# A list scheduler inside a kernel gets exact footprints, traced lengths, a shared port and another choice among ready instructions

## The chip, the cores and the metric

The kernel runs on one core of a Trainium2 chip. Five engines work side by side, each through its own queue, strictly in the order in which its instructions stand there: TensorE (PE, matrix products and the 128x128 transposes that are written as products), VectorE (DVE), ScalarE (ACT), GpSimd (POOL), and SyncE (SP), which here only issues transfers. An instruction that depends on another engine waits at the head of its queue for a semaphore, and what stands behind it waits with it. The metric is the device time of one execution in microseconds (us).

## What is computed

A first block of two layers and a second block of two layers, on 256 rows of width 1024, all in float32. The first block's layers have a mixer (layer 0: a dilated attention beside a gated linear recurrence, called RG-LRU; layer 1: pooling), an attention to 256 memory rows, and an MLP of width 4096. The second block's layers are, cut to what matters here:

```python
for l in range(DEPTH):
    h = x + 0.5 * swiglu(rms_norm_2(x, ffn1_norm[l]), ffn1_w1[l], ffn1_w3[l], ffn1_w2[l])
    n = rms_norm_2(h, mix_norm[l])
    p = n @ w_in[l]
    u_conv, q, k, v, q_mem = jnp.split(p, splits, axis=-1)
    y_conv = conv_module(u_conv, conv_w[l], conv_b[l], conv_ln_g[l], conv_ln_b[l])
    ...
    y_swa = sliding_window_attention(q, k, v, swa_sinks[l])
    ...
    y_mem = memory_attention(qm, mk, mv)
    y = jnp.concatenate([y_conv, y_swa, y_mem], axis=-1)
    h = h + y @ w_out[l]
    h = h + 0.5 * swiglu(rms_norm_2(h, ffn2_norm[l]), ffn2_w1[l], ffn2_w3[l], ffn2_w2[l])
    x = rms_norm_2(h, final_norm[l])

def conv_module(u, w_dw, b_dw, ln_g, ln_b):
    a, gate = jnp.split(u, 2, axis=-1)
    y = a * jax.nn.sigmoid(gate)
    y = lax.conv_general_dilated(
        y, w_dw[:, None, :], window_strides=(1,),
        padding=[(CONV_WIDTH_2 - 1, 0)],
        dimension_numbers=('NWC', 'WIO', 'NWC'),
        feature_group_count=CONV_CH) + b_dw
    y = layer_norm(y, ln_g, ln_b)
    return jax.nn.silu(y)
```

The convolution is depthwise, with 31 taps over 384 channels; q and k are normed and get rope. The part between `p = n @ w_in[l]` and `y @ w_out[l]` is called the mixer of the second block below; it occurs twice, for l = 0 and l = 1.

## The kernel before, in words

Every large product runs on PE in three terms. A float32 weight arrives by DMA as `raw`, ACT rounds it to `hi` (L303), DVE takes the rest `lo` = raw - hi (L304), and activations are split the same way (`h`, `put`, L367 on ACT and L368 on DVE). A product of a 128x128 block with 512 columns is then three matmuls, L325 to L327. Transposes are L384. So each weight costs PE, ACT and DVE time, and PE consumes them in program order of the products.

In a mixer of the second block, four pieces share the engines:

- The convolution. Its input `yp` lies with channels on the partitions. Seventeen of the 31 taps are multiply-adds on DVE into `cv` (3 at L1396, 48 at L1407, each 128x256). The other fourteen run as products on ACT into a buffer `pj` (39 at L1415) which POOL adds into `cv2` (39 at L1419). When all are done DVE adds the two sums (L1423, here called the merge), and a layer norm of each half of the rows follows (`ln`): transposes on PE, sums on ACT (L1437, L443), mean and scale on DVE (L1439 to L1444), a power on POOL (L426), three transposes back, tanh on ACT (L1451), products on DVE (L1454, L1458), and the put into the output projection's input.
- The projections to q, k, v with norms and rope, where POOL computes the powers (L426) and the rope's sums (L1210).
- The memory attention `m0 m1` and the sliding-window attention `s0 s1`. Each step goes from PE (scores) to DVE (L516 row maximum, L519), ACT (L529 exp), DVE (L538, L540), PE (transposes L384, products L1377 or L1343), and to a put (L367, L368).
- The output projection, K = 1024 = 8 blocks. Blocks 0 to 2 are the convolution's, 3 to 5 the window attention's, 6 and 7 the memory attention's. It adds into three PSUM tiles `acc` that are open at a time.

The order in the program is that of a string,

```python
ORDER = "c0 c1; k0 a0 a1 b0 b1 m0 m1 s0 s1 | t0; l0 | l1"
```

where `t0` are the taps and the chains between bars are emitted in turns. But this is not the order in which the engines get the work. The whole program is traced first, and then a list scheduler at its end writes all instructions anew. For every instruction it has the earlier ones that it must follow (`dependences`, from the footprints of its operands), a length in ns (`length`), and the tiles whose slots it needs. It walks in time, and on the engine that is free first it places, among the instructions that can start by its own reckoning, the one that is first in the program:

```python
        best = None
        for e in ENGINES:
            ...
                if best is None or at < best[0]:
                    best = (at, e)
        at, e = best
        ...
        i = heapq.heappop(now[e])
```

The order that it finds is fixed; on the chip each queue runs it whatever the real times are.

Of the kernel before, what the change touches and what calls it, by code (L numbers as in the profile page):

```python
# [24 lines left out]
D = 1024  # L25
# [6 lines left out]
class Slots:  # L32
    """tiles of a tag share a fixed number of slots"""
# [12 lines left out]
def footprint(ap):  # L46
    """(first, last) partition and element of a row that an access touches"""
    a = ap.bass_ap
    dims = list(ap.ap)
    step = dims[0][0]  # L50
    p0, f0 = divmod(a.offset, step) if step else (0, a.offset)
    f1 = f0 + sum((n - 1) * s for s, n in dims[1:]) + 1
    return a.tensor.name, (p0, p0 + dims[0][1], f0, f1)
# [9 lines left out]
def meet(a, b):  # L63
    return a[0] < b[1] and b[0] < a[1] and a[2] < b[3] and b[2] < a[3]


def inside(a, b):
    return b[0] <= a[0] and a[1] <= b[1] and b[2] <= a[2] and a[3] <= b[3]


def dependences(ops):
    """for every instruction the earlier ones that it must follow, its tiles, and those in PSUM"""
    writes, reads, matmul = {}, {}, {}
    before, tiles, banks = [], [], []
    for i, op in enumerate(ops):
# [13 lines left out]
        if op.engine == ENG.PE:  # L89
            # the groups of a PSUM bank one after the other  # L90
# [11 lines left out]
def length(op):  # L102
    """estimated time an instruction holds its engine, in ns"""
# [23 lines left out]

def list_schedule(ops, slots):
    """issue order: on every engine the first in the program among those that can start"""
# [8 lines left out]
    for i, ts in enumerate(slotted):  # L138
        for t in sorted(ts):
# [3 lines left out]
            users[t] += 1  # L143
    open_at = {tag: [0.0] * n for tag, n in slots.bufs.items()}
# [7 lines left out]
    bank_free = {}  # L152

    def offer(i):
# [5 lines left out]
        heapq.heappush(later[ops[i].engine], (at, i))  # L160
# [14 lines left out]
    while len(order) < len(ops):  # L175
        best = None
        for e in ENGINES:
            while later[e] and later[e][0][0] <= free[e]:
                heapq.heappush(now[e], heapq.heappop(later[e])[1])
# [5 lines left out]
        while later[e] and later[e][0][0] <= at:  # L185
            heapq.heappush(now[e], heapq.heappop(later[e])[1])
        i = heapq.heappop(now[e])
        # a PSUM bank takes one engine at a time
        clear = max((t for b in banks[i] for x, t in bank_free.get(b, {}).items() if x != e), default=0.0)
        if clear > at:  # L190
            heapq.heappush(later[e], (clear, i))
            continue
        order.append(i)
        if e == ENG.SP:
# [54 lines left out]
def kernel(ctx: ExitStack, tc: tile.TileContext, A: dict, out: bass.AP):  # L249
# [1356 lines left out]
```

## Time and profile before

| quantity | value |
|---|---|
| time, median of 3 runs | 1710.07 us (1709.3 to 1710.43) |
| the profiled execution, its span | 1709.7 us |
| PE busy | 1660.6 us, 97% of the span |
| DVE, ACT, POOL busy | 65%, 55%, 12% |
| transfers | 170 GB/s over the span, one queue on SP |

The span runs from the first to the last instruction that the profile holds. Matmuls overlap and their ends are modelled, so a PE that is called busy at half its clock counts as busy; the granted clock stands in a column of its own. Lines are named L1407 and so on, by the line of the kernel before; the changed kernel's body has the same lines 53 further down (L1407 is L1460 there).

### The profile page before, as it was taken

The page shows a single profiled execution, that of the slowest core. Times are in us where ns is not written, and L with a number is a line of the kernel's source. Part 1 is how long each engine was busy: PE and PEld are TensorE (multiplying, and loading weights), DVE is VectorE, ACT ScalarE, POOL GpSimd, SP SyncE. Part 2 cuts the span into 40 slices and gives each one's busy share as a digit, 9 for nine tenths or more (in the row PEclk, how much of TensorE's full clock was granted, in tenths as well). Part 3 has the DMA queues.
Part 4 walks back from the last instruction along what each step waited for, and adds up shares of the span by engine and source line. Part 5 has one row for each costly group of instructions (what it writes and reads, how often), then busy time and mean ns, then how long its engine had stood idle before and what let it go on. Part 6 is the DMA issues. An engine that isn't in the chain of part 4 may idle for free.

```text
span 1709.7 us, 22709 instructions
## 1 busy us (share of the span) xinstructions
PE 1660.6 (97%) x8144; PEld 1401.6 (82%) x8144; DVE 1118.7 (65%) x1717; ACT 942.3 (55%) x1685; POOL 210.7 (12%) x281
## 2 busy tenths in 40 slices
PE   8999999999999999999999799999999999799998
PEld 7878888888888888888888578888888888588886
DVE  7776475556556557656567996556665559975454
ACT  6675664445666445545456774445554447664343
POOL 2121100001010000100003910000200015520000
PEclk9999999999999999999999899999999999899999
DMA  9526355564634565655465155646655554355552
GB/s 298 183 98 195 114 187 174 184 223 158 195 117 148 185 198 167 214 172 180 162 208 174 37 148 178 217 154 208 222 178 170 170 192 136 86 165 168 198 166 92
DMA packets 159248, 291.44 MB, mean 170 GB/s; under 512 B 11040, under 2 KB 36128, under 8 KB 159136
## 3 DMA queue, kind: packets, MB, share of 16 engines
q1 hardware_dynamic: 159136, 290.00, 52.6%
q8 instruction: 64, 1.05, 0.2%
q14 instruction: 48, 0.39, 0.1%
HBM read 288.91 MB, written 1.05 MB: 170 GB/s over the span
## 4 chain that ended last, share of the span: by engine, by line
PE 90%; DVE 7%; ACT 2%; issue 1%; DMA 0%; POOL 0%; SPq 0%; POOLq 0%; DVEq 0%; ACTq 0%
PE acc L327 27%; PE acc L326 27%; PE acc L325 27%; PE tp L384 4%; DVE big L1407 3%; DVE lo L304 1%; PE sm L917 1%; PE sm L904 1%; PE sm L384 1%; PE acc L637 0%; DVE st L559 0%; PE acc L636 0%; PE acc L635 0%; DVE t L540 0%; PE sm L1327 0%
## 5 line engine op out<-in xcount | busy, mean ns | idle before, releaser
L325 PE MATMUL acc<-hi,h 128*128 128x512 f32 (+1 forms) x2048 | 786.1, 384 | 1.2 <-ACT h L367 1.2
L326 PE MATMUL acc<-lo,h 128*128 128x512 f32 (+1 forms) x2048 | 783.3, 383 | 0.9 <-DVE lo L304 0.9
L327 PE MATMUL acc<-hi,h 128*128 128x512 f32 (+1 forms) x2048 | 782.9, 383 | 0.0
L304 DVE TENSOR_TENSOR lo<-raw,hi 128x1024 fp32r<-128x1024 f32 (+2 forms) x570 | 652.2, 1160 | 149.1 <-ACT hi L303 136.2
L303 ACT CAST hi<-raw 128x1024 fp32r<-128x1024 f32 (+2 forms) x570 | 564.8, 1005 | 285.0 <-PE acc L327 243.8
L325 PEld LDWEIGHTS acc<-hi,h 128*128 128x128 f32 x2048 | 385.8, 188 | 67.0 <-ACT h L367 2.1
L326 PEld LDWEIGHTS acc<-lo,h 128*128 128x128 f32 x2048 | 385.6, 188 | 65.2 <-DVE lo L304 1.5
L327 PEld LDWEIGHTS acc<-hi,h 128*128 128x128 f32 x2048 | 385.5, 188 | 64.1 <-issue 0.7
L426 POOL TENSOR_TENSOR st<-st,nhalf 128x1 f32<-128x1 f32 (+2 forms) x74 | 66.9, 906 | 1429.5 <-DVE st L431 1227.4
L367 ACT CAST h<-tp 128x512 fp32r<-128x512 f32 (+1 forms) x80 | 45.1, 563 | 149.8 <-PE tp L384 149.8
L368 DVE TENSOR_TENSOR h<-tp,h 128x512 fp32r<-128x512 f32 (+1 forms) x80 | 53.0, 662 | 61.6 <-ACT h L367 61.5
L481 DVE SCALAR_TENSOR_TENSOR x<-acc,st,x 128x512 f32<-128x512 f32 x48 | 35.9, 748 | 85.4 <-PE acc L327 85.2
L443 ACT ACTIVATE t<-x 128x512 f32<-128x512 f32 x56 | 35.8, 638 | 97.2 <-DVE x L481 76.0
L384 PE MATMUL tp<-ident,t 128*128 128x128 f32 x488 | 76.1, 276 | 12.5 <-DVE t L1160 5.8
L384 PEld LDWEIGHTS tp<-ident,t 128*128 128x128 f32 x488 | 59.9, 141 | 30.2 <-DVE t L1160 6.6
L1116 DVE TENSOR_TENSOR t<-acc,t 128x512 f32<-128x512 f32 (+1 forms) x48 | 30.9, 643 | 80.0 <-PE acc L327 80.0
L1419 POOL TENSOR_TENSOR big<-big,big 128x256 f32<-128x256 f32 x78 | 66.4, 879 | 5.2 <-ACT big L1415 5.2
L325 PE MATMUL acc<-hi,big 128*128 128x512 f32 x160 | 64.3, 402 | 0.0
L326 PE MATMUL acc<-lo,big 128*128 128x512 f32 x160 | 64.1, 401 | 0.0
L1114 DVE SCALAR_TENSOR_TENSOR t<-t,acc 128x512 f32<-128x512 f32 (+1 forms) x48 | 30.8, 641 | 50.9 <-ACT t L1113 50.9
L1113 ACT ACTIVATE t<-acc,st 128x512 f32<-128x512 f32 (+1 forms) x48 | 31.1, 648 | 59.4 <-PE acc L327 54.0
L327 PE MATMUL acc<-hi,big 128*128 128x512 f32 x160 | 63.6, 398 | 0.0
(237 smaller groups left out, 1246.0 us busy)
## 6 DMA issues: line engine op xcount, KB each, us to landing
raw<-in_ffn_w_dram SPq DMA_DIRECT2D x208, 512.0 KB, 5.0
raw<-in_mlp_w_dram SPq DMA_DIRECT2D x128, 512.0 KB, 4.9
raw<-in_ffn_w_dram SPq DMA_DIRECT2D x64, 384.0 KB, 4.0
raw<-in_xa_w_kv_dram SPq DMA_DIRECT2D x32, 512.0 KB, 5.3
raw<-in_ev_w_in_dram SPq DMA_DIRECT2D x20, 512.0 KB, 5.6
raw<-in_w_in_dram SPq DMA_DIRECT2D x24, 384.0 KB, 4.8
raw<-in_xa_w_q_dram SPq DMA_DIRECT2D x16, 512.0 KB, 5.5
raw<-in_xa_w_o_dram SPq DMA_DIRECT2D x16, 512.0 KB, 5.6
```

The source lines that it names most:

```text
L303: nc.scalar.copy(hi[:, :n], raw[:, :n])
L304: nc.vector.tensor_tensor(out=lo[:, :n], in0=raw[:, :n], in1=hi[:, :n].bitcast(F32), op=ALU.subtract)
L325: nc.tensor.matmul(ps, l[0], r[0], start=start, stop=False)
L326: nc.tensor.matmul(ps, l[0], r[1], start=False, stop=False)
L327: nc.tensor.matmul(ps, l[1], r[0], start=False, stop=stop)
L367: nc.scalar.copy(h, src)
L368: nc.vector.tensor_tensor(out=self.lo(k0, n, t), in0=src, in1=h.bitcast(F32), op=ALU.subtract)
L384: nc.tensor.transpose(dst[:, i * P : i * P + rows], s_, ident[:rows, :rows])
L426: nc.gpsimd.tensor_tensor(out=dst, in0=src, in1=nhalf[:, :n], op=ALU.pow)
L481: nc.vector.scalar_tensor_tensor(x_, ps, scale, x_, op0=ALU.mult, op1=ALU.add)
L1407: nc.vector.scalar_tensor_tensor(cv[:, g], yp[:, g, 2 + j : 258 + j], col(cw, 93 * l + 3 * j + g), cv[:, g], op0=ALU.mult, op1=ALU.add,)
L1419: nc.gpsimd.tensor_tensor(out=cv2[:, g], in0=cv2[:, g], in1=pj[:, g], op=ALU.add)
```

## The change

All of it is in the scheduler. The instructions of the program, their operands and number, are the same. Comments and docstrings were also taken out; those lines are left out here.

```diff
 def footprint(ap):
     dims = list(ap.ap)
     step = dims[0][0]
     p0, f0 = divmod(a.offset, step) if step else (0, a.offset)
-    f1 = f0 + sum((n - 1) * s for s, n in dims[1:]) + 1
-    return a.tensor.name, (p0, p0 + dims[0][1], f0, f1)
+    runs, width = [0], 1
+    for s, n in reversed(dims[1:]):
+        if n > 1 and s == width and len(runs) == 1:
+            width *= n
+        elif n > 1 and s:
+            runs = [r + i * s for i in range(n) for r in runs]
+    runs = tuple(sorted((f0 + r, f0 + r + width) for r in runs))
...
 def length(op):
         rows = free(ins[0])
         full = ins[0].dtype == F32
+        if ins[0].dtype == F32R:
+            return rows / 2.4 + 13.5
         return rows * ((2 if op.is_transpose else 4) if full else 1) / 2.4 + 3
...
+def shares_port(op):
+
+    if op.engine == ENG.Pool:
+        return True
+    ins = [x for x in on_chip(op.ins) if math.prod([n for _, n in list(x.ap)[1:]]) > 1]
+    if op.engine != ENG.DVE or any(x.bass_ap.space == PSUM for x in ins):
+        return False
+    return len(ins) > 1 or type(op).__name__ != "InstTensorReduce"
...
 def list_schedule(ops, slots):
+    heirs = [[] for _ in ops]
+    for tag, n in slots.bufs.items():
...
+        for old, new in zip(names, names[n:]):
+            for i in by[old]:
+                heirs[i].append(by[new][0])
+    key = [len(ops)] * len(ops)
+    for i in reversed(range(len(ops))):
+        if ops[i].engine == ENG.PE:
+            key[i] = i
+        else:
+            key[i] = min([key[j] for j in after[i] + [h for h in heirs[i] if h > i]], default=len(ops))
+    rank = [0] * len(ops)
+    for r, i in enumerate(sorted(range(len(ops)), key=lambda i: (key[i], i))):
+        rank[i] = r
...
-        i = heapq.heappop(now[e])
+        r, i = heapq.heappop(now[e])
...
+        if port[i]:
+            clear = port_free[ENG.Pool if e == ENG.DVE else ENG.DVE]
+            if clear > at:
+                heapq.heappush(later[e], (clear, r, i))
+                continue
         order.append(i)
+        if port[i]:
+            port_free[e] = at + cost[i]
```

In words: two accesses now meet only where their runs of elements meet, not where the intervals around them do. A product of rounded operands is reckoned 13.5 ns longer than its columns, before 3 ns. POOL's instructions and DVE's on SBUF alone (reductions excepted) are reckoned to exclude each other. And among the instructions that can start, an engine takes the one with the smallest `key`: the place in the program of the earliest matmul that depends on it, directly, through other instructions, or because it frees a slot that a later tile waits for.

What that does to the queues is seen at three places. The first is POOL's queue in the mixer of layer 0 (`big_8260` is `cv2`, the other `big` are the buffers `pj`, `st` and `t` are factors and rope values of the projections and attentions). Before, from the third power on:

```order
L1419 TENSOR_TENSOR big_8260<-big_8260,big_8577 128x256 x3
L426 TENSOR_TENSOR st_8448<-st_8444,nhalf 128x2
L426 TENSOR_TENSOR st_8464<-st_8460,nhalf 128x6
L1210 TENSOR_TENSOR t_1845_8452<-t_1845_8452,t_1854_8476 128x3x64
L1210 TENSOR_TENSOR t_1867_8547<-t_1867_8547,t_1868_8549 128x128
L1210 TENSOR_TENSOR t_1866_8546<-t_1866_8546,t_1874_8565 128x3x64
L1419 TENSOR_TENSOR big_8260<-big_8260,big_8645 128x256 x2
L1210 TENSOR_TENSOR t_1866_8546<-t_1866_8546,t_1875_8570 128x3x64
L1419 TENSOR_TENSOR big_8260<-big_8260,big_8645 128x256
L1419 TENSOR_TENSOR big_8260<-big_8260,big_8700 128x256
L426 TENSOR_TENSOR st_8542<-st_8538,nhalf 128x2
```

And now, in the same stretch:

```order
L479 TENSOR_TENSOR st_8448<-st_8444,nhalf 128x2
L1263 TENSOR_TENSOR t_1845_8452<-t_1845_8452,t_1853_8471 128x3x64
L1263 TENSOR_TENSOR t_1845_8452<-t_1845_8452,t_1854_8476 128x3x64
L1263 TENSOR_TENSOR t_1867_8547<-t_1867_8547,t_1868_8549 128x128
L1263 TENSOR_TENSOR t_1866_8546<-t_1866_8546,t_1874_8565 128x3x64
L479 TENSOR_TENSOR st_8542<-st_8538,nhalf 128x2
L1263 TENSOR_TENSOR t_1866_8546<-t_1866_8546,t_1875_8570 128x3x64
L479 TENSOR_TENSOR st_8464<-st_8460,nhalf 128x6
L479 TENSOR_TENSOR st_8661<-st_8657,nhalf 128x4
L479 TENSOR_TENSOR st_8558<-st_8554,nhalf 128x6
L479 TENSOR_TENSOR st_8716<-st_8712,nhalf 128x4
L1472 TENSOR_TENSOR big_8260<-big_8260,big_8483 128x256 x2
```

Only four adds (three of `big_8433`, one of `big_8483`) now stand ahead of the last power of the projections, and 35 behind it. On ACT the products that feed them moved too: those of `big_8818`, `big_8834` and `big_8859`, nine in all, now stand behind the CAST of the last put of the window attention and one weight CAST.

The second place is DVE's queue around the merge of the same mixer (`sm_8841` and `sm_8883` are tiles of the memory attention, `sm_9065` the last of the window attention). Before:

```order
L304 TENSOR_TENSOR lo_9189<-raw_9187,hi_9188 128x1024
L368 TENSOR_TENSOR h_1922_8772<-sm_8841,h_1921_8771 128x128
L1423 TENSOR_TENSOR big_8259<-big_8259,big_8260 128x768
L368 TENSOR_TENSOR h_1922_8772<-sm_8883,h_1921_8771 128x128
L536 TENSOR_TENSOR st_8932<-st_8932,st_8937 128x4
L516 TENSOR_REDUCE st_8967<-sm_8961 128x2
```

Now:

```order
L593 TENSOR_SCALAR t_1985_9066<-t_1985_9066,st_9086 128x256 x2
L357 TENSOR_TENSOR lo_9227<-raw_9225,hi_9226 128x512
L421 TENSOR_TENSOR h_1922_8772<-sm_9065,h_1921_8771 128x128
L357 TENSOR_TENSOR lo_9423<-raw_9421,hi_9422 128x1024
L1476 TENSOR_TENSOR big_8259<-big_8259,big_8260 128x768
L1492 TENSOR_SCALAR st_9108<-st_9106 128x1
```

The merge stood ahead of nearly the whole window attention and now stands behind its last put. Counted from the first tap, 135 DVE instructions stood ahead of it, and 207 do now.

The third place is PE's queue at the end of that mixer (`tp_9101`, `tp_9134`, `tp_9119` and `tp_9152` are the layer norm's transposes, `acc_9231` and `acc_9273` tiles of the output projection, `h_1955` its input from the convolution). Before, the transposes stood apart:

```order
L384 MATMUL tp_9119<-ident,t_1994_9105 128x128 x3
L327 MATMUL acc_9231<-hi_9181,h_1922_8772 128x512
L326 MATMUL acc_9273<-lo_9201,h_1921_8771 128x512
L384 MATMUL sm_9029<-ident,t_1976_9030 128x128 x4
L327 MATMUL acc_9273<-hi_9200,h_1922_8772 128x512
```

Now all twelve stand together, behind the window attention's last product:

```order
L1396 MATMUL sm_9065<-t_1985_9066,v_1755_8083 64x128 x4
L378 MATMUL acc_9321<-hi_9181,h_1921_8771 128x512
L379 MATMUL acc_9321<-lo_9182,h_1921_8771 128x512
L380 MATMUL acc_9321<-hi_9181,h_1922_8772 128x512
L437 MATMUL tp_9101<-ident,big_8259 128x128 x3
L437 MATMUL tp_9134<-ident,big_8259 128x128 x3
L437 MATMUL tp_9119<-ident,t_1994_9105 128x128 x3
L437 MATMUL tp_9152<-ident,t_2005_9138 128x128 x3
L378 MATMUL acc_9231<-hi_9188,h_1955_8955 128x512
```

Behind them come 51 matmuls of the output projection's open tiles, the first of which reads the convolution's part. Layer 1's mixer has the same three patterns.

Outside the mixers less moves. In the first block, the two POOL products of the RG-LRU (L746, L747, each 128x1024) stood between the powers of the memory attention's keys, and now stand behind all of them. Near the program's start, in the pooling layer and in the memory attentions, instructions of DVE and ACT change places with weight splits. The rest of the program keeps its order but for small swaps.

## Rows read from the trace of the kernel before

**Rows 1.** The page: span, PE, and the clock granted in 40 slices.

```profile
span 1709.7 us, 22709 instructions
PE 1660.6 (97%) x8144; PEld 1401.6 (82%) x8144; DVE 1118.7 (65%) x1717; ACT 942.3 (55%) x1685; POOL 210.7 (12%) x281
...
PEclk9999999999999999999999899999999999899999
```

**Rows 2.** The page: the chain that ended last, by engine.

```profile
PE 90%; DVE 7%; ACT 2%; issue 1%; DMA 0%; POOL 0%; SPq 0%; POOLq 0%; DVEq 0%; ACTq 0%
```

**Rows 3.** Stretches: us; busy (count) of PE, PEld, DVE, ACT, POOL; clock; DMA share, GB/s.

```profile
118.10:124.10 6.00, 6.00 (x17) 4.84 (x17) 5.41 (x9) 1.14 (x4) 1.60 (x1) 0.50 0.24 90
...
927.00:960.00 33.00, 28.96 (x141) 24.46 (x140) 32.87 (x78) 24.86 (x54) 24.78 (x28) 1.00 0.36 116
960.00:967.20 7.20, 4.67 (x23) 3.13 (x21) 7.20 (x20) 5.11 (x14) 6.96 (x8) 1.00 0.00 0
967.20:987.70 20.50, 14.38 (x55) 10.22 (x55) 20.50 (x40) 10.48 (x29) 14.32 (x20) 0.50 0.10 27
987.70:1011.00 23.30, 22.65 (x150) 16.56 (x150) 22.41 (x91) 18.62 (x62) 3.13 (x4) 1.00 0.53 159
...
1430.00:1490.00 60.00, 46.21 (x237) 35.72 (x236) 59.62 (x143) 43.20 (x114) 42.24 (x51) 0.86 0.26 75
```

**Rows 4.** PE's waits, 110 to 126 us and 925 to 1012 us.

```profile
PE tp L384 <- DVE t L869: 3.8, 1, 3.8
...
PE tp L384 <- DVE t L1160: 2.9, 1, 2.9
```

**Rows 5.** Timeline of POOL and DVE behind the wait at 114 us.

```profile
113.39 2.86 POOL L747 TENSOR_TENSOR h<-h,h 128x1024 f32<-128x1024 f32 x1
...
113.96 2.33 DVE L559 TENSOR_SCALAR st<-st,st 128x2 f32<-128x2 f32 x1
```

**Rows 6.** Groups in 927 to 990 us: count, busy us, mean ns.

```profile
L1407 DVE SCALAR_TENSOR_TENSOR big<-big,G,big 128x256 f32<-128x256 f32 x48 | 30.5, 671 | 0.0
...
L1419 POOL TENSOR_TENSOR big<-big,big 128x256 f32<-128x256 f32 x39 | 33.2, 879 | 2.6 <-ACT big L1415 2.6
...
L1415 ACT ACTIVATE big<-big,G 128x256 f32<-128x256 f32 x39 | 17.1, 503 | 1.0 <-POOL big L1419 0.9
```

**Rows 7.** Line L1407 in both mixers: ns, shortest, median, longest.

```profile
L1407 DVE SCALAR_TENSOR_TENSOR big<-big,G,big x96: 465/479/1043, 928.8 to 1474.9; 128x256 f32<-128x256 f32 x96
```

**Rows 8.** Timeline of the first mixer's convolution, its merge, and the last put.

```profile
927.83 1.05 DVE L1396 TENSOR_SCALAR big<-big,G 128x256 f32<-128x256 f32 x3
...
966.60 8.28 POOL L1419 TENSOR_TENSOR big<-big,big 128x256 f32<-128x256 f32 x11
...
989.30 0.95 DVE L1423 TENSOR_TENSOR big<-big,big 128x768 f32<-128x768 f32 x1
...
1010.01 0.28 DVE L368 TENSOR_TENSOR h<-sm,h 128x128 fp32r<-128x128 f32 x1
```

**Rows 9.** Timeline, 990 to 1010 us: the steps of the layer norm.

```profile
994.20 0.49 ACT L1437 ACTIVATE t<-tp 128x384 f32<-128x384 f32 x1
994.97 1.09 ACT L303 CAST hi<-raw 128x1024 fp32r<-128x1024 f32 x1
...
997.83 0.58 ACT L443 ACTIVATE t<-t 128x384 f32<-128x384 f32 x1
...
999.57 1.00 POOL L426 TENSOR_TENSOR st<-st,nhalf 128x1 f32<-128x1 f32 x1 [17.36 <-DVE st L1439]
1001.75 0.55 PE L384 MATMUL tp<-ident,t 128*128 128x128 f32 x3
...
1004.09 1.04 DVE L1454 TENSOR_SCALAR t<-tp,hg 128x128 f32<-128x128 f32 x3
...
1006.16 1.16 ACT L1451 ACTIVATE t<-tp,hg 128x128 f32<-128x128 f32 x3 [0.38 <-PE tp L384]
...
1009.61 0.51 ACT L367 CAST h<-t 128x384 fp32r<-128x384 f32 x1
```

More of the change, by code (lines that the diff above doesn't have):

```diff
@@ L51, in footprint @@
     p0, f0 = divmod(a.offset, step) if step else (0, a.offset)
-    f1 = f0 + sum((n - 1) * s for s, n in dims[1:]) + 1
-    return a.tensor.name, (p0, p0 + dims[0][1], f0, f1)
+    runs, width = [0], 1
[5 more added lines that the diff above has]
+    runs = tuple(sorted((f0 + r, f0 + r + width) for r in runs))
+    if len(runs) > 16:
+        runs = ((runs[0][0], runs[-1][1]),)
+    return a.tensor.name, (p0, p0 + dims[0][1], runs)
 def on_chip(aps):
@@ L63, in meet @@
 def meet(a, b):
-    return a[0] < b[1] and b[0] < a[1] and a[2] < b[3] and b[2] < a[3]
+    if a[0] >= b[1] or b[0] >= a[1]:
+        return False
+    return any(x[0] < y[1] and y[0] < x[1] for x in a[2] for y in b[2])
 def inside(a, b):
-    return b[0] <= a[0] and a[1] <= b[1] and b[2] <= a[2] and a[3] <= b[3]
+    return b[0] <= a[0] and a[1] <= b[1] and all(any(y[0] <= x[0] and x[1] <= y[1] for y in b[2]) for x in a[2])
 def dependences(ops):
@@ L125, in length @@
     return math.prod([k for _, k in list(outs[0].ap if outs else op.ins[0].ap)]) * 4 / 360
+def shares_port(op):
[3 more added lines that the diff above has]
+    if op.engine != ENG.DVE or any(x.bass_ap.space == PSUM for x in ins):
+        return False
+    return len(ins) > 1 or type(op).__name__ != "InstTensorReduce"
 def list_schedule(ops, slots):
@@ L143, in list_schedule @@
             users[t] += 1
+    heirs = [[] for _ in ops]
+    for tag, n in slots.bufs.items():
+        names = list(queue[tag])
+        by = {t: [] for t in names}
+        for i, ts in enumerate(slotted):
+            for t in ts:
+                if slots.tag[t] == tag:
+                    by[t].append(i)
+        for old, new in zip(names, names[n:]):
[10 more added lines that the diff above has]
+        rank[i] = r
     open_at = {tag: [0.0] * n for tag, n in slots.bufs.items()}
@@ L152, in list_schedule @@
     bank_free = {}
+    port = [shares_port(op) for op in ops]
+    port_free = {ENG.DVE: 0.0, ENG.Pool: 0.0}
     def offer(i):
@@ L159, in offer @@
         at = max([ready_at[i]] + [held[t] for t in slotted[i]])
-        heapq.heappush(later[ops[i].engine], (at, i))
+        heapq.heappush(later[ops[i].engine], (at, rank[i], i))
     def place(tag):
@@ L178, in list_schedule @@
             while later[e] and later[e][0][0] <= free[e]:
-                heapq.heappush(now[e], heapq.heappop(later[e])[1])
+                heapq.heappush(now[e], heapq.heappop(later[e])[1:])
             if now[e] or later[e]:
@@ L185, in list_schedule @@
         while later[e] and later[e][0][0] <= at:
-            heapq.heappush(now[e], heapq.heappop(later[e])[1])
-        i = heapq.heappop(now[e])
+            heapq.heappush(now[e], heapq.heappop(later[e])[1:])
+        r, i = heapq.heappop(now[e])
         clear = max((t for b in banks[i] for x, t in bank_free.get(b, {}).items() if x != e), default=0.0)
         if clear > at:
-            heapq.heappush(later[e], (clear, i))
+            heapq.heappush(later[e], (clear, r, i))
             continue
+        if port[i]:
+            clear = port_free[ENG.Pool if e == ENG.DVE else ENG.DVE]
+            if clear > at:
+                heapq.heappush(later[e], (clear, r, i))
+                continue
         order.append(i)
+        if port[i]:
+            port_free[e] = at + cost[i]
         if e == ENG.SP:
```

## The prediction

> **What bounds the kernel now.** The page comes first. PE is busy for 1660.6 of 1709.7 us and its clock is full but in one slice of 40 [rows 1]; nine tenths of the chain that ended last are PE's own work, DVE has 7% and the transfers nothing [rows 2]. So a new order can win only where PE stands still or runs at half its clock, and it loses where it makes PE do so. Then I looked for these places by stretches [rows 3]. They are few. From 927 to 987.7 us, the first mixer of the second block, PE is idle for 4.0, 2.5 and 6.1 us (length less busy), and 20.5 us pass at a granted clock of 0.50 (1.2 of 2.4 GHz), where 14.38 us of busy time do the work of 7.2: about 20 us lost. The second mixer, 1430 to 1490 us, has 13.8 us idle and a mean clock of 0.86, that is 16.8 us at half clock with some 70% of it busy, so 6 more: 20 again. The third place is one wait of 3.8 us at 114 us [rows 4], behind which 6.0 us run at half clock [rows 3].
>
> In both mixers DVE is the engine that has no pause: 32.87 of 33, 7.20 of 7.20 and 20.50 of 20.50 us [rows 3]. There the reader is to see that a tap on DVE takes 0.465 us at its shortest and 0.671 in the mean [rows 6, 7]: it is slower where POOL's adds run beside it.
>
> **The first block: a gain.** At 114 us PE waits for DVE's L869. DVE had spent 2.33 us in a tiny 128x2 instruction, which ran while POOL was in the 2.86 us product L747 [rows 5]. The change puts L746 and L747 behind the four powers, so L869's factor comes without them. That removes the wait, 3.8 us, and with it the stretch at half clock, 6.0 us that do the work of 3.0: 6.8 us. What is late next is the RG-LRU's result, which the first output projection needs only some 20 us on, behind the memory's products, which PE has in store. If that cover were gone, the 2.86 and 2.40 us of the two products would come back; so the term lies between -6.8 and -1.5. I take -6.8.
>
> **The mixers: a loss.** Here I follow one mixer, in the times of layer 0.
>
> First, when does the window attention end? From the first tap at 927.83 to the merge at 989.30 [rows 8], 61.5 us, DVE does 135 instructions. Each taken at the shortest that the trace has for its form, less the 0.07 us by which neighbours overlap, they sum to 44.2 us. The other 17.3 came with 39 adds on POOL, 0.44 us for an add. (From rows alone, 48 taps at 0.671 - 0.465 are 9.9 us, 0.25 an add, and the longest tap less the median is 0.56 [rows 6, 7]: the bounds.) In the new order DVE has 206 instructions from the first tap to the last put of the window attention; the same sum gives 58.0 us. Thirty adds can run beside them (39 less the nine whose products stand behind the put): 13.3 us at 0.44. With 2 us for waits between DVE, ACT and PE inside a softmax, the last put is done at 927.8 + 58.0 + 13.3 + 2 = 1001 us, against 1010.3 before [rows 8]. Bounds: 993.4 (0.25 an add, no waits) and 1007 (0.56, 4 us of waits). So the attention does get faster, by 9 us.
>
> Second, what comes then? Before, the convolution was done at 989.30 + 0.95, and the layer norm went on beside the window attention, so that PE was busy for 22.65 of 23.3 us from 987.7 to 1011 [rows 3]. Now ACT has, behind the put's CAST, a weight CAST of 1.09 us [rows 9] and then nine products; the first is done after some 0.5 us [rows 6], at about 1002.3. POOL needs 8.28 / 11 = 0.75 us an add [rows 8], longer than a product, so nine adds end at 1009.1, if POOL has caught up: 26 adds stand between the last power and these nine, 23 us at their mean of 0.879 [rows 6], and the old last power lay ahead of the add at 966.60 [rows 8], so POOL is through by 990 and waits for ACT. The merge takes 0.95: 1010. Then the layer norm by its steps [rows 8, 9]: transposes 0.55, sum 0.49, squares 0.58, power 1.00, transposes 0.55, products 1.04, tanh 1.16, CAST 0.51, together 5.9; four DVE steps of 384 columns (mean off, scale, product, put) at half the merge's 0.95, 1.9; and a dozen hand-overs between engines with the second half of the rows between them, some 2. That is 10 us, not under 8, and not over the 20 that it took before between other work (989.30 to 1009.61). PE's queue has nothing to put under it: the twelve transposes stand together, and the matmul behind them reads the layer norm's result. So PE goes on at 1020 us, with 51 matmuls left before the next norm. Before, it had that many left at 1011 us, where the stretch of rows 3 ends. The loss is 9 us.
>
> Third, the clock. A wait of 3.8 us was followed by 6.0 us at 0.50 [rows 3, 4], which cost 3.0; here PE stands for almost 20 us, so I add 3.0. What the old mixer lost by its clock lies ahead of 1011 us and is counted already. A mixer thus costs 12 us; the bounds are +1.4 (993.4 + 19 = 1012.4, clock kept) and +22 (put at 1007, 12 us of layer norm, clock lost). Both mixers have the same order: +24.
>
> **What else moves.** Idle PE time outside these places is 49.1 (1709.7 less 1660.6) less 27.1 in the mixers (4.0, 2.5, 6.1, 0.7 and 13.8) and 3.8: 18.2 us, much of it the first loads and the last rows, whose order hardly changes. The start now takes four input loads ahead of the first weight, for or against by a microsecond or two. The pooling layer and the memory attentions may win as much. I take -1, between +2 and -4. The exact footprints and the new matmul length cost nothing by themselves; they act through the order alone.
>
> **Sum.** 1709.7 + 24 - 6.8 - 1 = 1725.9 us. The profile's own time is 0.4 under the median of the runs, so 1726 us.
>
> **Rivals.**
>
> *The attention wins more than the convolution loses (faster).* The old mixer lost 20 us of PE, and the new order takes the attention out from behind the taps: the first row maximum of the memory attention came late because DVE was in taps. For it speaks that the queue of POOL has the powers free of adds. The point from which it decides is the last put: some 19 us later PE goes on, so that a mixer breaks even at a put at 992 (989 if the clock falls). Against it stands that DVE's 206 instructions alone need until 985.8, with no wait for POOL. At a put at 990, 3 us for the clock, the mixers cost 2 together: 1704 us; with no loss by the clock and a put at 986, 1690. Chance 0.26.
>
> *The two blocks cancel (same).* At 0.25 us an add and 1 us of waits the put comes at 994.5, PE goes on at 1013.5, the clock holds for most of it, and the mixers cost 7 together against 7.8 gained elsewhere: 1709 to 1710 us. Chance 0.10.
>
> *POOL holds DVE for the whole add (slower still).* Where each of the thirty adds stops DVE for its 0.75 us, they cost 22.6, not 13.3: the put comes at 1010, PE goes on at 1029, and a mixer costs 21: 1744 us. A tap beside an add takes up to 1.04 us against 0.48 [rows 7], which is 0.56 and not 0.75, so I give it 0.12. The Trainium skill says of this, on the page "SBUF — State Buffer", section "Who interferes with whom", that a DVE instruction with two inputs in SBUF and a GpSimd instruction that reads SBUF exclude each other for the whole instruction; by that rule the time would be the 1744 us of this rival, and the mean of the rows stays under it.
>
> *The order doesn't act in the first block.* The RG-LRU's result is late instead, and 5 of the 6.8 us come back: 1731 us, inside the forecast's own range.
>
> **How the numbers follow.** The forecast, a mixer that costs 4 to 16 us, has 0.52, with a range of its own from 1714 to 1736. With the third rival that makes 0.64 for slower by over 0.2% (3.4 us, which is about what a measurement of this kernel can tell from no change), 0.10 for the same, 0.26 for faster. The range takes in the same case, the upper half of the faster one and the lower end of the third: 1698 to 1742 leaves some 0.2 out.
>
> **What would show it.** In the new profile: the wait at 114 us gone and the clock full there; in each mixer the first row maximums and the last put of the window attention earlier by some 9 us (1001 in old times); POOL's adds in one row to the end, the merge 8 to 10 us behind the last put; then PE's longest waits of the whole program, for the merge and for the layer norm's steps, near 20 us in each mixer, with half clock behind them. The prediction is wrong if the last put comes before 992 or if PE's waits behind it are under 12 us; its size is wrong if POOL still has a backlog of adds when the last product arrives.

## The result and the profile after

The changed kernel took 1739.8 us (median of 4, 1736.48 to 1741.46) against 1710.25 us before (1709.3 to 1710.91): a ratio of 1.0174, 95% interval 1.0162 to 1.0186. It is 29.6 us slower; 1726 had been forecast. The execution that was profiled is the fastest of the four, 1736.48 us with a span of 1734.7, so the profiles differ by 25.0 us and 3 to 5 us of the medians' difference lie between executions.

The page of the changed kernel, span, busy time and clock, answers to [rows 1]:

```profile
span 1734.7 us, 22734 instructions
PE 1659.6 (96%) x8144; PEld 1397.2 (81%) x8144; DVE 1106.7 (64%) x1717; ACT 944.6 (54%) x1685; POOL 186.0 (11%) x281
...
PEclk9999999999999999999999879999999999889999
```

DVE and POOL are busy for less than before, 1106.7 us against 1118.7 and 186.0 against 210.7 (the page before), and the kernel is slower: this is read as time that the two take from each other less than before, and PE pays for it. Where, PE's waits over the whole program say (waiting instruction, what it waited for, us in total, times, longest):

```profile
PE sm L437 <- DVE t L593: 14.7, 7, 5.9
PE tp L437 <- DVE big L1476: 12.7, 2, 9.4
PE acc L378 <- ACT h L420: 10.5, 7, 2.8
PE tp L437 <- DVE t L1497: 5.4, 2, 2.7
```

The second and fourth are the layer norm's transposes, waiting for the merge and for the scaled rows; they did not wait before. The third holds two waits of 2.8 us for the layer norm's result. The first is a softmax in the attentions, with a wait of 5.9 us in each mixer; before it had 5.8 us in all:

```profile
PE sm L384 <- DVE t L540: 5.8, 2, 2.9
```

Of the wait of 3.8 us at 114 us [rows 4] 0.9 is left.

To see how much each part of the program gained or lost, the start of a PE instruction in the profile is compared with the work that lies ahead of it on PE, each instruction taken at its pitch at full clock (0.227 us for a product of 512 columns). The difference is PE's lost time up to there: waits, half clock and the start. This is worked out from the records, not printed by a view, and what is used below are its differences between kernels and between columns; the columns are the amounts of work in us. The first block's mixer is behind by 140, the first mixer of the second block lies between 900 and 960, the second between 1240 and 1440.

```
lost time at work of     140    900    960   1240   1440
before                  24.6   31.4   54.1   55.2   78.4
changed kernel          15.6   24.9   63.5   66.3  103.5
```

The first block gains 9.0 us and has 6.5 left at 900. The mixers lose 38.6 and 37.2 us where they lost 22.7 and 23.2: 15.9 and 14.0 us more. With 1.7 us between them that is the 25.0 us of the profiles (-6.5 + 15.9 + 1.7 + 14.0).

The first mixer on the timeline, with the steps of the forecast (start, length, engine and line; the bracket is idle time ahead of it and what ended it):

```profile
921.46 1.06 DVE L1449 TENSOR_SCALAR big<-big,G 128x256 f32<-128x256 f32 x3
...
998.81 0.29 DVE L421 TENSOR_TENSOR h<-sm,h 128x128 fp32r<-128x128 f32 x1 [1.15 <-ACT h L420]
...
1008.20 0.96 DVE L1476 TENSOR_TENSOR big<-big,big 128x768 f32<-128x768 f32 x1 [6.07 <-POOL big L1472]
...
1001.42 6.74 POOL L1472 TENSOR_TENSOR big<-big,big 128x256 f32<-128x256 f32 x9 [1.11 <-ACT big L1468]
...
1000.78 3.69 ACT L1468 ACTIVATE big<-big,G 128x256 f32<-128x256 f32 x9
...
1009.21 1.54 PE L437 MATMUL tp<-ident,big 128*128 128x128 f32 x6 [9.43 <-DVE big L1476]
...
1013.47 1.51 PE L437 MATMUL tp<-ident,t 128*128 128x128 f32 x6 [2.72 <-DVE t L1497]
...
1017.81 0.80 PE L378 MATMUL acc<-hi,h 128*128 128x512 f32 x1 [2.82 <-ACT h L420]
```

The first tap starts 6.4 us earlier than before [rows 8]. From there to the last put 77.6 us pass, from the put to the merge 9.1, from the merge to the matmul with which PE goes on 9.6: nine products, nine adds, the merge and the layer norm in one line, with PE idle but for the layer norm's own transposes. The stretches (as in [rows 3]) show the rest:

```profile
921.46:999.10 77.64, 62.80 (x343) 48.18 (x342) 71.19 (x206) 51.05 (x133) 38.70 (x43) 0.93 0.33 96
...
1000.00:1017.80 17.80, 3.05 (x12) 2.17 (x12) 7.10 (x17) 9.62 (x25) 8.29 (x13) 0.51 0.16 46
1017.80:1019.80 2.00, 1.99 (x5) 1.61 (x6) 1.64 (x4) 0.51 (x1) 0.99 (x2) 0.50 0.00 0
1019.80:1021.80 2.00, 2.00 (x8) 1.59 (x7) 0.00 (x0) 0.00 (x0) 0.00 (x0) 0.71 0.00 0
```

PE is busy for 3.05 of 17.8 us. When it goes on its clock is at 0.50 for 2 us and then, by the mean of 0.71, for 1.2 more: 3.2 us that do the work of 1.6. DVE, which had hardly a pause before (81.44 of the 82.46 us from the first tap to the last put), is idle for 6.45 us ahead of the put (77.64 less 71.19). DVE's waits in that stretch:

```profile
DVE st L569 <- PE sm L1417: 2.5, 3, 1.9
DVE h L421 <- ACT h L420: 1.5, 2, 1.1
DVE lo L357 <- ACT hi L356: 1.2, 1, 1.2
```

The longest is for a score product of PE, which came to it at half clock (0.50 from 960 to 965 us) behind its own wait of 5.9 us for a softmax. Most of the rest is for ACT, near the end of the attention.

The second mixer does not repeat this. Its last put, merge, last adds and products, and PE behind them, and then the stretch from its first tap to its last put:

```profile
1513.45 0.29 DVE L421 TENSOR_TENSOR h<-sm,h 128x128 fp32r<-128x128 f32 x1 [2.07 <-ACT h L420]
...
1516.72 0.94 DVE L1476 TENSOR_TENSOR big<-big,big 128x768 f32<-128x768 f32 x1
...
1508.18 7.54 POOL L1472 TENSOR_TENSOR big<-big,big 128x256 f32<-128x256 f32 x10 [1.26 <-ACT big L1468]
...
1511.83 0.92 ACT L1468 ACTIVATE big<-big,G 128x256 f32<-128x256 f32 x2
...
1513.15 0.27 ACT L420 CAST h<-sm 128x128 fp32r<-128x128 f32 x1
...
1517.72 1.54 PE L437 MATMUL tp<-ident,big 128*128 128x128 f32 x6 [3.27 <-DVE big L1476]
...
1526.32 0.79 PE L378 MATMUL acc<-hi,h 128*128 128x512 f32 x1 [2.83 <-ACT h L420]
```

```profile
1432.71:1513.74 81.03, 65.58 (x343) 50.40 (x342) 71.27 (x190) 54.12 (x142) 43.78 (x51) 0.89 0.31 92
```

So the first of the three patterns of layer 0 is in layer 1 only in part: the last products stand ahead of the last put's CAST, not behind it, and the last ten adds run around the put. The merge is only 3.0 us behind the put. But the put comes 81.0 us behind the first tap, where the kernel before had 81.2, so this attention is hardly faster; DVE is idle for 9.8 us ahead of the put. PE's waits behind the put are 15.0 us in the first mixer (9.43, 2.72 and 2.82) and 8.8 in the second (3.27, 2.72 and 2.83).

Last, the groups of the taps and the adds in the first mixer, beside [rows 6] (the last column is idle time of the engine just before them):

```profile
L1460 DVE SCALAR_TENSOR_TENSOR big<-big,G,big 128x256 f32<-128x256 f32 x48 | 24.8, 559 | 0.0
...
L1472 POOL TENSOR_TENSOR big<-big,big 128x256 f32<-128x256 f32 x39 | 31.8, 844 | 25.2 <-ACT big L1468 25.2
```

A tap is shorter than before, 559 ns against 671. But POOL now waits 25.2 us for ACT's products, before 2.6: the adds were not late by POOL's own work, their products came late from ACT's queue. For the same reason the shorter tap says little: 12 of the 39 adds start before the last tap ends, before all 39 did.

### The profile page after: what moved, and what is told of

The parts are those of the page before. It is cut to its first block, busy times and chain, and to the rows that moved or that the text cites. A ratio compares the mean times of both kernels' runs of the same rounds, so it can differ in the third digit from the quotient of the medians.

```text
span 1734.7 us, 22734 instructions
## 1 busy us (share of the span) xinstructions
PE 1659.6 (96%) x8144; PEld 1397.2 (81%) x8144; DVE 1106.7 (64%) x1717; ACT 944.6 (54%) x1685; POOL 186.0 (11%) x281
## 4 chain that ended last, share of the span: by engine, by line
PE 88%; DVE 5%; ACT 3%; issue 1%; DMA 1%; POOL 1%; SPq 0%; POOLq 0%; ACTq 0%; DVEq 0%
PE acc L378 26%; PE acc L380 26%; PE acc L379 26%; PE tp L437 4%; DVE lo L357 1%; ACT hi L356 1%; PE sm L970 1%; PE sm L957 1%; PE sm L437 1%; DMA raw<-in_ffn_w_dram 1%; DMA raw<-in_w_in_dram 1%; PE acc L688 1%; PE acc L690 1%; PE acc L689 0%; PE sm L1417 0%
## 5 line engine op out<-in xcount | busy, mean ns | idle before, releaser
L479 POOL TENSOR_TENSOR st<-st,nhalf 128x1 f32<-128x1 f32 (+3 forms) x74 | 65.3, 885 | 1442.5 <-DVE st L484 1228.9
L1472 POOL TENSOR_TENSOR big<-big,big 128x256 f32<-128x256 f32 x78 | 62.6, 832 | 47.6 <-ACT big L1468 47.6
L378 PE MATMUL acc<-hi,big 128*128 128x512 f32 x160 | 63.4, 396 | 0.0
L430 ACT ACTIVATE t<-tp,G 128x128 f32<-128x128 f32 x208 | 60.2, 382 | 5.9 <-PE tp L437 3.2
```

The lines of the kernel that those rows point to most:

```text
L378: nc.tensor.matmul(ps, l[0], r[0], start=start, stop=False)
L430: nc.scalar.activation(r_[:, sl], src[:, sl], AF.Copy, scale=g)
L479: nc.gpsimd.tensor_tensor(out=dst, in0=src, in1=nhalf[:, :n], op=ALU.pow)
L1472: nc.gpsimd.tensor_tensor(out=cv2[:, g], in0=cv2[:, g], in1=pj[:, g], op=ALU.add)
```

## The experiments

The question was what in the change makes the mixers lose. The forecast had put it down to the merge's place behind the attention, and left open which of the four parts put it there.

**The parts one by one.** The key alone:

```diff
+    heirs = [[] for _ in ops]
+    key = [len(ops)] * len(ops)
...
-        heapq.heappush(later[ops[i].engine], (at, i))
+        heapq.heappush(later[ops[i].engine], (at, rank[i], i))
```

> The scheduler of before with the new key alone: old footprints, old matmul length, no shared port. In the order that comes out the merge stands ahead of the window attention's last put again (117 DVE instructions behind the first tap; before 135, in the changed kernel about 163 and behind the last put). Theory A, that the loss comes from the layer norm having no work beside it on PE: the two mixers lose what they lost before (some 20 us each), the gain of the first block stays, 1697 to 1710 us. Rival B, that taking attention work first is what costs, whatever the merge's place: 1725 to 1740 us, with PE's lost time again some 15 us larger in each mixer.

The new length alone:

```diff
         full = ins[0].dtype == F32
+        if ins[0].dtype == F32R:
+            return rows / 2.4 + 13.5
```

> The scheduler of before with the new matmul length alone. The order of the second mixers comes out as in the run with the first block alone. If the length is the small loss there: 1712 to 1717 us (two mixers with 2 to 3 us more each, and 1 to 2 us between them). If the footprints are: 1708 to 1712 us.

The shared port alone:

```diff
+        if port[i]:
+            clear = port_free[ENG.Pool if e == ENG.DVE else ENG.DVE]
+            if clear > at:
+                heapq.heappush(later[e], (clear, i))
+                continue
         order.append(i)
+        if port[i]:
+            port_free[e] = at + cost[i]
```

> The scheduler of before with the shared port alone. If the port is the loss by itself: each mixer loses 33 to 40 us in place of 23, and the first block gains nothing, 1730 to 1748 us, with PE waiting more than 10 us in one piece for a factor that comes through POOL. If it needs the key, the footprints or the length beside it: under 1722 us.

The footprints alone (`footprint`, `meet` and `inside` as in the change):

> The scheduler of before with the exact footprints alone, the fourth part by itself. The order of the second mixers is nearly that of before. If the parts of the change are told apart by now, this one does little: 1706 to 1712 us, with some 23 us lost in each mixer. If exact footprints free enough in the first block to move its waits: 1700 to 1705 us, or, by a longer wait at 114 us, 1713 to 1718 us.

And the change less one part. Without the key:

```diff
-    for r, i in enumerate(sorted(range(len(ops)), key=lambda i: (key[i], i))):
+    for r, i in enumerate(range(len(ops))):
```

> The changed scheduler with the first in the program taken again among the ready ones, so exact footprints, new length and the shared port stay. The merge stands ahead of the last put. Theory A: mixers as before, 1704 to 1714 us; the wait at 114 us may stay, since the two large POOL products stand ahead of two powers again. Rival C, that the shared port in the reckoning is the cause: 1725 us or more, with the mixers slow. Rival B (the key): no more than before, 1700 to 1712 us.

Without the port:

```diff
-    port = [shares_port(op) for op in ops]
+    port = [False] * len(ops)
```

> The changed scheduler without the shared port; footprints, length and key stay. The merge stands ahead of the last put (98 DVE instructions behind the first tap). Theory A: 1695 to 1710 us. Rival B (the key costs by itself): 1725 us or more. Rival C (the shared port is the cause by itself): 1695 to 1710 us too, told apart by the run without the key.

Measured, with the ratio to before on the same chip, its interval, and the lost time by the profile as above:

```
                     median us  ratio [95%]               140    900    960   1240   1440
key alone             1709.84   1.0003 [0.9994, 1.0013]  19.7   26.3   50.4   51.4   77.5
footprints alone      1711.64   1.0013 [1.0004, 1.0023]  22.1   28.1   51.8   52.8   77.6
length alone          1722.23   1.0077 [1.0061, 1.0092]  22.6   32.3   57.6   60.3   87.2
shared port alone     1740.66   1.0182 [1.0168, 1.0195]  21.1   28.4   70.5   71.7  108.7
all without the port  1720.51   1.0068 [1.0053, 1.0083]  19.5   28.9   55.8   58.9   86.4
all without the key   1745.92   1.0217 [1.0202, 1.0232]  27.4   36.6   75.4   78.1  113.0
```

The shared port alone makes the kernel as slow as the whole change, and taking it out of the change gives 19 of the 30 us back; the mixers then lose 26.9 and 27.5 us, before 22.7 and 23.2. None of the three ranges written down for that run holds its 1720.51 us. The key alone changes nothing that can be measured, gains in the first block and gives it back, and helps by 6 us where the port is reckoned (without it 1745.92). The footprints do nearly nothing. The length alone, which was meant to make the reckoning truer, costs 12.8 us, over both ranges written down for it. The profiled execution has 8.8 of them, small in each place: 2.6 and 3.7 us more in the mixers (25.3 and 26.9) and the rest between and ahead of them. At a work of 140 it is 2.0 us ahead of the kernel before, although its wait at 114 us is longer. PE's waits in that run, 60 to 140 us and 930 to 1030 us:

```profile
PE tp L386 <- DVE t L871: 5.2, 1, 5.2
...
PE sm L386 <- DVE t L542: 4.2, 3, 2.8
PE tp L386 <- DVE t L1162: 3.2, 1, 3.2
```

The first and the last are those of before, 3.8 and 2.9 us [rows 4], each a bit longer. Which of the instructions that the length moves does that was not tried.

**The merge ahead of the attention.** The convolution's instructions ranked by their own place in the program, all else as in the change:

```diff
-        if ops[i].engine == ENG.PE:
+        if ops[i].engine == ENG.PE or tiles[i] & slots.conv:
             key[i] = i
...
+            slots.conv.add(b_.tensor.name)
```

> The changed scheduler, but the instructions of the convolution (taps, products, adds, merge and the layer norm's first transposes) are ranked by their own place in the program and not by the matmul that waits for them. All else keeps the key. The merge stands ahead of the last put. Theory A: each mixer is back at some 20 us lost, the first block keeps its 7 to 10 us: 1695 to 1708 us. Rival B: the attention is still chosen by the key, so 1725 us or more. Rival C: the same, since the shared port is still reckoned.

1737.78 us, ratio 1.0164 [1.0147, 1.0181]. Theory A falls: the merge, at 1000.46 us, stands 13 us ahead of the last put, and the mixers lose 39.6 and 37.7 us all the same, only in another place. PE's waits in this run, 920 to 1045 us, and then rows of its timeline:

```profile
PE tp L438 <- DVE t L1325: 19.6, 2, 17.9
PE sm L438 <- DVE t L594: 6.8, 2, 6.2
```

```profile
946.92 0.71 POOL L480 TENSOR_TENSOR st<-st,nhalf 128x2 f32<-128x2 f32 x1 [0.24 <-DVE st L603]
...
972.43 2.71 POOL L1475 TENSOR_TENSOR big<-big,big 128x256 f32<-128x256 f32 x3 [16.50 <-ACT big L1471]
...
970.19 1.69 ACT L357 CAST hi<-raw 128x1024 fp32r<-128x1024 f32 x2 [16.16 <-DMA raw<-in_w_out_dram]
...
959.37 4.43 DVE L1463 SCALAR_TENSOR_TENSOR big<-big,G,big 128x256 f32<-128x256 f32 x11
963.72 5.83 DVE L358 TENSOR_TENSOR lo<-raw,hi 128x1024 fp32r<-128x1024 f32 x6
...
971.27 1.83 DVE L358 TENSOR_TENSOR lo<-raw,hi 128x1024 fp32r<-128x1024 f32 x2 [1.31 <-ACT hi L357]
...
975.84 0.22 DVE L613 TENSOR_SCALAR st<-st,st 128x2 f32<-128x2 f32 x1
976.16 0.29 DVE L1325 TENSOR_TENSOR t<-t,st 128x128 f32<-128x128 f32 x1
```

PE waits 17.9 us for the rows that DVE scales in L1325 at 976.16 us, by a factor from L613. The power that this factor needs was done on POOL at 947.63, 28 us before: there are two such powers and two such factors in the mixer, the other factor was made at 946.02, and POOL's next power ended only behind 975.84. So PE does not wait for POOL. The scaling stands in DVE's queue behind eleven taps, eight weight splits and sixteen small products for the rope (L1242 and L1243, between the rows shown), and DVE goes through them from 959.37 us on with one pause, 1.31 us for a rounded weight.

That pause is the end of a chain. The splits free buffers of raw weights, and SP's queue waits 28.1 us for a split before it issues the next loads (the waits of SP, 940 to 975 us, below). So the load arrives late, and ACT stands 16.16 us at the head of its queue with a weight CAST; behind it are the products for which POOL waits 16.50 us. Of all this only the 1.31 us reach the wait of 17.9. No single instruction is slow: the order has put what PE needs first behind work that could have waited.

```profile
SPq L356 <- DVE lo L358: 30.8, 3, 28.1
```

The runs without the key and with the port alone have a wait of this kind too: the last instructions of DVE ahead of its end are again taps, splits and rope products, and POOL's powers were done long before. PE's waits there, 920 to 1045 us and the whole program:

```profile
PE tp L437 <- DVE st L612: 17.8, 1, 17.8
```

```profile
PE tp L403 <- DVE st L578: 34.1, 2, 17.8
```

With the key this wait becomes the one of the changed kernel: the powers and what hangs on them go ahead, the adds and products to the end.

**Which direction of the port.** In the scheduler, DVE and POOL that ask for the port at the same time are served in the order of the list of engines, where DVE comes first, and a DVE that has no pause asks again at the very time at which it lets go. So in the reckoning POOL gets a turn only when DVE has nothing ready that takes the port. This is read from the code; the reckoned times were not looked at. Two runs take the two directions apart:

```diff
-        if port[i]:
+        if port[i] and e == ENG.DVE:
             clear = port_free[ENG.Pool if e == ENG.DVE else ENG.DVE]
```

> The changed scheduler, where DVE still waits for POOL on the shared port but POOL never waits for DVE. Theory D, that the shared port harms because in the reckoning DVE has no pause and POOL hardly gets a turn, so that the adds and with them ACT's products move to the end of the mixer, while on the chip POOL runs its add in 0.75 to 0.88 us whatever DVE does: the adds are spread over the mixer in this order, the mixers lose some 20 to 27 us each, 1703 to 1722 us. Rival E, that reckoning the two engines one after the other is wrong in either direction: 1730 us or more.

```diff
-        if port[i]:
+        if port[i] and e == ENG.Pool:
             clear = port_free[ENG.Pool if e == ENG.DVE else ENG.DVE]
```

> The other half: POOL waits for DVE, DVE never waits for POOL. Theory D: the queues of the mixers come out almost as in the changed kernel (27 adds in one row behind the last power), so 1732 to 1746 us. Rival E: the same or a little better, since one direction of the wait is gone, 1715 to 1735 us.

With POOL never waiting: 1726.0 us, 1.0098 [1.0084, 1.0112]. With DVE never waiting: 1738.12 us, 1.0166 [1.0152, 1.0180]. Beside 1720.5 without the port, POOL's wait in the reckoning costs 17.6 us and DVE's 5.5. The group of the adds in the first mixer, first of the one and then of the other run:

```profile
L1472 POOL TENSOR_TENSOR big<-big,big 128x256 f32<-128x256 f32 x39 | 28.8, 768 | 2.9 <-ACT big L1468 2.9
```

```profile
L1472 POOL TENSOR_TENSOR big<-big,big 128x256 f32<-128x256 f32 x39 | 32.6, 865 | 20.0 <-ACT big L1468 20.0
```

Where POOL waits in the reckoning, it stands 20.0 us on the chip for its products, as in the change (25.2); where it doesn't, 2.9, as before (2.6). So theory D holds for the larger part. It had 1703 to 1722 us for the first of the two runs, and 1726 is over that: DVE's wait has a price of its own, which D did not have. The second run lies in the range of D and over that of E, 1715 to 1735 us.

**A key with the chain's length, without the port.**

```diff
+    cost = [length(op) for op in ops]
+    total = sum(c for op, c in zip(ops, cost) if op.engine == ENG.PE)
...
+            t -= cost[i]
+            key[i] = t
...
-            key[i] = min([key[j] for j in after[i] + [h for h in heirs[i] if h > i]], default=len(ops))
+            key[i] = min(
+                [key[j] for j in after[i] + [h for h in heirs[i] if h > i]], default=total
+            ) - cost[i] - 200
+    port = [False] * len(ops)
```

> The changed scheduler without the shared port and with a key that is a latest start: the reckoned time of the waiting matmul less the lengths of all that stands between. If the key without a chain's length is what makes the run without the port 11 us slower than before, the long convolution goes first and the mixers lose 20 us each or less: 1695 to 1708 us. If the length of the chain doesn't matter: 1715 to 1725 us, as without it.

1719.6 us, 1.0059 [1.0043, 1.0074]: not to be told from the 1720.51 without the port. The chain's length in the key is not what was missing.

**The first block alone.** Key and port for the first block, neither for the second:

```diff
+    slots.second = len(nc.cur_bb.bb.instructions) - first
...
-    for r, i in enumerate(sorted(range(len(ops)), key=lambda i: (key[i], i))):
+    for r, i in enumerate(sorted(range(len(ops)), key=lambda i: (key[i] if i < slots.second else i, i))):
...
-    port = [shares_port(op) for op in ops]
+    port = [shares_port(op) and i < slots.second for i, op in enumerate(ops)]
```

> The changed scheduler with the key and the shared port for the instructions of the first block alone; in the second block the first in the program is taken and no port is reckoned (footprints and length stay everywhere). If the change's gain in the first block (PE's lost time 6.5 us under before at the end of it) and the loss of the mixers are independent of each other: the mixers as in the kernel before, 1700 to 1706 us, faster than both. If the footprints and the new length cost by themselves in the mixers (the run without the port was 11 us over before): 1708 to 1714 us.

1714.25 us, 1.0029 [1.0018, 1.0041]: the first block is as good as in the change, but the mixers lose 25.0 and 26.5 us, as with the length alone. So the last run also gives the second block its old footprints and length:

```diff
-        if ins[0].dtype == F32R:
+        if ins[0].dtype == F32R and not second:
             return rows / 2.4 + 13.5
...
+        if i >= second:
+            rd, wr = [interval(x) for x in rd], [interval(x) for x in wr]
```

> The new scheduler's four parts for the first block, the old footprints, length, choice and no port for the second, in one pass. If the second block's new footprints and length are what took the gain from the run with the first block alone (its mixers lost 25.0 and 26.5 us, before 22.7 and 23.2): PE's lost time 6 us under before, 1701 to 1706 us, faster than before. If the first block's gain is given back later whatever the second block's rules are: 1707 to 1713 us.

1703.4 us, 0.9962 [0.9950, 0.9975]: faster than both kernels, by 0.4% against the one before, with an interval that leaves out 1. Lost time by its profile, and its waits between 90 and 145 us:

```
lost time at work of     140    900    960   1240   1440
first block new          16.5   25.5   50.5   53.6   80.1
and second block old     16.7   23.1   45.6   47.1   70.7
```

```profile
PE tp L445 <- DVE t L930: 0.9, 1, 0.9
```

The mixers are back at 22.5 and 23.6 us, and of the first block's gain 7.7 us are there at the end by the profiles; the medians differ by 6.1.

## Why the prediction was right, and where it was not

*The first block.* Forecast -6.8 for the RG-LRU and -1 elsewhere; the profile has -9.0 at a work of 140 and -6.5 when the second block's mixers begin. The wait of 3.8 us is down to 0.9, and the clock is full from 110 to 125 us:

```profile
PE tp L437 <- DVE t L922: 0.9, 1, 0.9
```

```profile
110.00:125.00 15.00, 14.08 (x66) 11.28 (x65) 10.05 (x14) 11.02 (x19) 5.50 (x3) 1.00 0.52 164
```

The runs by parts show that this needs the key: without it 27.4 us are lost by 140, with it alone 19.7, before 24.6. The other parts alone gain 2.0 to 3.5 us up to there.

*The mixers.* The place and the order of size were right, and in the first mixer the mechanism on the chip too: the attention is not hidden behind taps any more, and the nine adds, the merge and the layer norm have nothing under them. In the second mixer the path was another one. The pieces, in us; the fifth row is the time from the first tap to the same point of PE's work in the kernel before:

```
                               reckoned    first   second
first tap to last put             73.2     77.64    81.03
last put to merge                  8.1      9.10     2.98
merge to PE's next product        10.9      9.61     9.60
sum                               92.2     96.35    93.61
kernel before, same work          83.2     82.10    81.97
later by                           9.0     14.25    11.64
half clock behind it               3.0      1.6      1.6
cost of the mixer                 12       15.9     14.0
```

The last row is the measured one, by the lost time; the two rows above it give 15.9 and 13.2. The term that was mis-sized most is the first: 2 us were reckoned for waits inside the softmaxes, and DVE stands for 6.45 and 9.8 us. So the attention is done 4.8 us earlier than before in the first mixer and 0.2 us in the second, not 9. The contention was right in the first mixer (58.0 + 13.3 = 71.3 us, measured 71.19 busy). The point of comparison was 1.1 us off (PE had the same work left at 1009.9 us, not at 1011), and the clock cost half of what was reckoned.

In the second mixer the nine products and adds are not behind the put, so the term that the forecast has for them, 8.1 us, was 3.0, and the longer attention made up for it. That its 14.0 us came out near 12 is luck. The prediction named a sign by which it would be wrong, PE's waits behind the put under 12 us: they are 15.0 us in the first mixer and 8.8 in the second, so by its own sign the mechanism fails there. Why DVE waits longer in the second mixer (4.3 us for ACT's CASTs of the puts) was not tried. The time of 1739.8 us lies over the range of the forecast itself, 1714 to 1736, and within 1698 to 1742, which takes in the lower end of the third rival; of the difference 3 us and more lie between executions of the changed kernel. The page of the kernel before has two slices of 40 below full clock [rows 1], one for each mixer, where the prediction read one.

*The reason behind it.* The forecast tied the loss to the merge's place behind the attention. This is what one sees in the first mixer of the changed kernel, but moving the merge does not win the time back: with the merge ahead the mixers lose as much, in a wait of 17.9 us for rows that DVE scales late. What the loss hangs on in the runs by parts is the shared port in the reckoning. Alone it costs 31 us, and without it the change still costs 11. That it works by making POOL late in the reckoning fits the rule of the scheduler and the two runs with one direction each; it was not seen in reckoned times. The sentence that the footprints and the length cost nothing by themselves was nearly right for the first. The length alone gives an order that costs 12.8 us, a term that the forecast did not have.

*The rivals.* POOL holding DVE for the whole of an add was given 1744 us. The time came near that, but not in this way: the thirty adds cost DVE 13.2 us in the first mixer (71.19 less 58.0), 0.44 each and not 0.75, and the put came at 1005.5 us in the old times, not 1010. By the rule of "SBUF — State Buffer", section "Who interferes with whom", in the Trainium skill, which was cited there, a tap and an add exclude each other for their whole length; this 0.44 us of an add, too, stays under that.

## What to carry to other kernels

A list scheduler's order runs on queues that wait at their heads, so what a reckoned conflict gets wrong is not its own length but what is queued behind it. Look at who is starved in a resource model, check it against the trace (here: does POOL's add really wait for DVE?), and test each rule alone and on each stretch of the program: here the same rules gained 6.5 us up to the second block and lost 30 in its mixers, and keeping them for the first block alone was 6.1 us faster than the kernel before. And when a wait is found, follow it to the instruction that ended it: a long wait on a neighbouring queue at the same time need not be its cause.

## What the runs showed of the hardware that was not expected

Of a tap and an add that run side by side DVE pays more than POOL. The adds of the changed kernel, then of the kernel before (ns, shortest, median, longest):

```profile
L1472 POOL TENSOR_TENSOR big<-big,big x78: 717/744/1777, 932.7 to 1515.0; 128x256 f32<-128x256 f32 x78
```

```profile
L1419 POOL TENSOR_TENSOR big<-big,big x78: 713/900/1688, 934.5 to 1474.9; 128x256 f32<-128x256 f32 x78
```

The nine adds in one row, beside a DVE that does next to nothing, take 6.74 us, 0.75 each. In the kernel before, beside a DVE busy for all but 1 us, an add takes 879 ns in the mean [rows 6], 166 over its shortest, with single ones up to 1688. A tap takes 465 ns at its shortest [rows 7] and 671 in the mean, and all 39 adds cost DVE 17.3 us there by the sum of the prediction, 0.44 us for an add.

PE's clock fell within a us of PE's last product ahead of the merge: it is 1.00 from 990 to 1000 us, with PE pausing several times, and 0.51 in the mean from 1000.0 to 1017.8, with PE busy for 3.05 us of it. It was full again 3.2 us after PE went on. After the shorter wait of 3.8 us at 114 us in the kernel before it had taken 6.0 us [rows 3]. So in these two places the price of a wait in clock is not in proportion to the wait.
